# The first B tile moved from the hardware queues to the software queue, and the left half of B loaded by half tiles, in a matmul with RMS norm

## The chip, the cores and the metric

The kernel runs on one core of one Trainium2 chip. The metric is device time in microseconds (us) of one execution. The profile gives a span, from the first to the last instruction of one execution; in all profiled runs the timed value of that execution is 1.8 us above its span, so a change of the span is a change of the time.

Names used below. TensorE is the matrix engine (PE in the profile), DVE the vector engine, ACT the scalar engine, POOL the GpSimd engine, SP the sync engine. A *hardware queue* is a queue of DMA transfers issued by SP or ACT; the *software queue* is issued by POOL, and in this kernel every load that converts float32 to bf16 on its way goes by it. A load has *landed* when the last of the 16 DMA engines has written its share.

## The reference

```python
def reference(a, b, gamma, eps):          # a, b: 2048 x 2048 float32
    x = np.matmul(a, b)
    rms = np.sqrt(np.mean(x ** 2, axis=-1, keepdims=True) + eps)
    return (gamma * x / rms).astype(np.float32)
```

## The kernel before

The output has 16 row blocks of 128 rows. The first four are the *head*: they are multiplied while B is still being loaded, so that TensorE has work from the start. The contraction of 2048 is cut into 8 tiles of 256 rows (kp 0 to 7). In the left half (output columns 0 to 1023), each stage needs 512 KB of A and 1 MB of B, both counted as float32 in memory; in the right half only the 1 MB of B. After the head about 160 us of products follow, which read B from on-chip memory.

How the first tile comes in, before the change. The A tile of kp 0 is one load on the sync queue. The B tile of kp 0 comes as two float32 loads on the scalar queue and is cast to bf16 by DVE and ACT:

```python
    nc.sync.dma_start(out=a0f, in_=a[0:HB * P, 0:W2].rearrange("(r p) k -> p r k", p=P))
    for t in range(2):
        nc.scalar.dma_start(out=b0f[t], in_=b[t * P:(t + 1) * P, 0:HALF])
```

All other tiles come by the software queue, one load of 1 MB for each tile of B (512 KB once written as bf16):

```python
    def load_b(j, kp):
        nc.gpsimd.dma_start(
            out=raw[j][kp],
            in_=b[kp * W2:(kp + 1) * W2, j * HALF:(j + 1) * HALF].rearrange(
                "(t p) n -> p t n", p=P))

    def load_head(kp):
        nc.gpsimd.dma_start(out=ah(kp), in_=a[0:HB * P, kp * W2:(kp + 1) * W2] ...)   # cut
        load_b(0, kp)
```

The loop over the left half issues loads four tiles ahead, then the matmuls:

```python
    for kp in range(KP):
        if kp + 4 < KP:
            load_head(kp + 4)
        else:
            load_later(1)           # a tile of the right half, load_b(1, ...)
        ...                         # transpose the next A tile, then the stage's matmuls
```

The last stage of the right half (kp 7) does the two products of a later pair first (`acc<-b,s` and `acc<-early,s` in the profile), then the eight plain matmuls, then one more `acc<-early,s`. That last one closes the head; I use its start as the end of the head.

```python
        if kp == KP - 1:
            for m in (2, 5):
                pair_matmul(m, kp)          # needs the B tile of kp 7
            pair_matmul(1, kp - 1)
        for g, kt in order:
            head_matmul(banks[g], *g, kt)   # eight, two halves of the tile
        ...
            pair_matmul(1, kp)              # the end of the head
```

Eleven warm-up matmuls on zeros run from 1.46 us, so that the throttle grants TensorE its full clock before real work comes.

## Time and profile before

| | us |
|---|---|
| timed, median of the first 3 runs | 222.82 (222.45 to 223.10) |
| timed, median of all 6 runs of the comparison | 222.53 (222.14 to 223.10) |
| span of the profiled execution (itself timed at 222.97) | 221.2 |
| TensorE busy | 210.0, 95% of the span |

From the page of the kernel before, the busy times and three of the DMA queues (queue, kind: packets, MB written, share of the 16 engines' time):

```profile
PE 210.0 (95%) x1035; PEld 97.7 (44%) x1035; DVE 167.4 (76%) x330; ACT 128.1 (58%) x263; POOL 29.4 (13%) x59
...
q0 software_dynamic: 9936, 23.33, 41.7%
q10 hardware_dynamic: 432, 1.31, 2.0%
q8 instruction: 8, 0.13, 0.2%
```

TensorE is 95% busy, which tempts one to think that loads don't matter. They do in the first 57 us. The timeline of TensorE of the kernel before, at the end of the head (start us, duration us, engine, line, operation, out<-in, shapes, count):

```profile
56.44 0.38 PE L289 MATMUL acc<-early,s 128*128 128x512 bf16 x1
56.69 0.59 PE L289 MATMUL acc<-b,s 128*128 128x512 bf16 x2
...
59.05 0.38 PE L289 MATMUL acc<-early,s 128*128 128x512 bf16 x1
```

The last tile of the right half landed at 56.64 us, and the stage that needs it starts at 56.69. The head ends at 59.05. The chain of waits of the kernel before (start us, length us, what) shows the same from the left half: a load to 25.05, and right after it the matmuls that needed it.

```profile
7.35 17.70 DMA b<-in_b_dram
25.05 0.04 issue
25.10 1.67 PE acc L384 x7
```

In the right half a stage takes TensorE about 2.4 us and a tile about 2.5 us to load.

The start of the kernel before, in the timeline of all engines (the bracket is the idle time before the instruction and what ended it):

```profile
5.16 0.74 DVE L158 CAST b<-early 128x512 bf16<-128x512 f32 x1 [1.28 <-DMA early<-in_b_dram]
6.40 0.63 PE L155 MATMUL tbank<-t_left,early 128*128 128x128 f32 x4 [0.53 <-DMA early<-in_a_dram]
7.54 2.88 PE L384 MATMUL acc<-b,head_at 128*128 128x512 bf16 x12
```

The A tile lands at 6.26, the halves of the B tile at 5.13 and 8.68, and the first real matmul starts at 7.54. The rate of the loads in that time, from the view by stretches of the kernel before (stretch, its length, then busy us and instructions of each engine, granted clock, DMA share, GB/s written). The software queue writes bf16, half of what it reads, so 205 GB/s of a B load are 410 GB/s of source:

```profile
5.00:6.00 1.00, 0.87 (x4) 0.10 (x2) 0.74 (x1) 0.62 (x1) 1.00 (x2) 1.00 1.12 337
6.00:7.00 1.00, 0.60 (x6) 0.63 (x7) 0.00 (x0) 0.00 (x0) 1.00 (x10) 1.00 0.78 196
...
12.00:16.00 4.00, 3.94 (x26) 1.93 (x24) 0.69 (x1) 0.58 (x1) 1.46 (x2) 1.00 1.24 205
```

From 6 to 7 us 196 GB/s were written, mostly float32 by the scalar queue, so the loads ran at half of the 410 GB/s that they reach from 12 us on. The change aims at this first stretch.

### The profile page before, as it was taken

The numbers are of one execution on the slowest core, as the hardware profiler recorded it, in microseconds if no ns is written. First come the engines' busy times: TensorE is split into PE (matmuls) and PEld (weight loads), VectorE is DVE, ScalarE is ACT, GpSimd is POOL, SyncE is SP. The second block draws the span as 40 slices with busy tenths as digits, with TensorE's granted clock in tenths as the row PEclk, the third lists the DMA queues.
The fourth block names the chain that finished last, engine by engine and source line by source line (L and its number), as shares of the span: only waits on it lengthen the run. The fifth ranks groups of instructions, "written<-read, shape, count | busy, mean of one in ns | idle before, by whom it ended". The sixth has DMA issues, their size and how long they took to land.

```text
span 221.2 us, 3022 instructions
## 1 busy us (share of the span) xinstructions
PE 210.0 (95%) x1035; PEld 97.7 (44%) x1035; DVE 167.4 (76%) x330; ACT 128.1 (58%) x263; POOL 29.4 (13%) x59
## 2 busy tenths in 40 slices
PE   7899899999999999999999999999999999999950
PEld 2445454444455444444444444444444444444430
DVE  2428789999988898969696639855794759797691
ACT  3110001830698898678945997389738995334570
POOL 7634323220000001200110002000200000000040
PEclk9999999999999999999999999999999999999996
DMA  6999999999938596956799249955798349044045
GB/s 184 223 202 209 203 208 210 211 211 238 426 114 357 187 291 120 316 230 150 219 308 397 79 88 266 367 221 95 187 302 367 69 90 381 32 190 193 1 190 191
DMA packets 36321, 47.13 MB, mean 213 GB/s; under 512 B 21969, under 2 KB 26065, under 8 KB 34897
## 3 DMA queue, kind: packets, MB, share of 16 engines
q0 software_dynamic: 9936, 23.33, 41.7%
q1 hardware_dynamic: 25936, 22.29, 33.6%
q10 hardware_dynamic: 432, 1.31, 2.0%
q8 instruction: 8, 0.13, 0.2%
q14 instruction: 9, 0.07, 0.1%
HBM read 34.60 MB, written 16.78 MB: 232 GB/s over the span
## 4 chain that ended last, share of the span: by engine, by line
PE 83%; DMA 8%; POOL 3%; DVE 2%; issue 1%; ACT 1%; DVEq 0%; ACTq 0%; POOLq 0%
PE acc L289 69%; PE acc L384 12%; DMA b<-in_b_dram 8%; POOL early L105 1%; POOL b L99 1%; DVE x L709 1%; PE tbank L415 1%; PE tbank L172 1%; DVE x L712 1%; ACT sq L307 0%; PE tbank L189 0%; PE acc L189 0%; DVE a L709 0%; ACT sq L778 0%; DVE x L786 0%
## 5 line engine op out<-in xcount | busy, mean ns | idle before, releaser
L289 PE MATMUL acc<-b,s 128*128 128x512 bf16 x408 | 92.1, 379 | 0.0
L289 PEld LDWEIGHTS <-s 128*128 128x128 f16 (+1 forms) x512 | 49.9, 98 | 59.9 <-DVE s L264 0.4
L384 PE MATMUL acc<-b,head_at 128*128 128x512 bf16 x176 | 41.9, 379 | 1.0 <-DMA b<-in_b_dram 0.9
L307 ACT ACTIVATE sq<-x 128x512 bf16<-128x512 f32 x54 | 34.0, 630 | 6.9 <-DVE x L709 3.0
L366 DVE SCALAR_TENSOR_TENSOR x<-x,r,gamma_sb 128x1024 f32<-128x1024 f32 x28 | 34.8, 1281 | 0.7
L223 ACT ACTIVATE sq<-a 128x1024 bf16<-128x1024 f32 x24 | 25.3, 1054 | 2.4 <-DMA a<-in_a_dram 1.9
L384 PEld LDWEIGHTS <-head_at 128*128 128x128 bf16 x176 | 16.8, 98 | 20.6 <-issue 1.9
L246 ACT ACTIVATE head_at<-a,s 128x2048 f16<-128x2048 f32 x10 | 20.0, 1998 | 3.7 <-DVE s L233 3.7
L426 ACT COPY x<-acc 128x512 f32<-128x512 f32 x6 | 3.4, 586 | 25.7 <-PE acc L384 25.7
L289 PEld LDWEIGHTS <-head_at 128*128 128x128 f16 (+1 forms) x112 | 10.9, 98 | 13.2
L289 PE MATMUL acc<-early,head_at 128*128 128x512 bf16 x64 | 14.5, 379 | 0.0
L289 PEld LDWEIGHTS <-at_even 128*128 128x128 f16 x96 | 9.4, 98 | 11.3
L289 PE MATMUL acc<-early,s 128*128 128x512 bf16 x56 | 14.4, 379 | 0.0
L264 DVE TENSOR_TENSOR s<-head_at 128x1024 f16<-128x1024 f16 (+5 forms) x22 | 13.4, 635 | 0.1
L596 DVE TENSOR_TENSOR x<-x,x 128x512 f32<-128x512 f32 x9 | 6.2, 692 | 8.8 <-ACT x L594 8.3
L99 POOL DMA_DIRECT2D b<-in_b_dram x15 | 10.6, 706 | 16.0 <-DMA b<-in_b_dram 13.4
L578 ACT COPY x<-acc 128x512 f32<-128x512 f32 x9 | 5.2, 574 | 11.6 <-PE acc L289 11.5
L289 PE MATMUL acc<-t_left,s 128*128 128x512 bf16 x48 | 11.3, 379 | 0.0
L280 DVE TENSOR_TENSOR b<-b 128x1024 bf16<-128x1024 bf16 x16 | 10.8, 684 | 0.2
L289 PE MATMUL acc<-t_left,head_at 128*128 128x512 bf16 x48 | 10.9, 379 | 0.0
L289 PE MATMUL acc<-t_left,at_even 128*128 128x512 bf16 x48 | 10.8, 379 | 0.0
L289 PE MATMUL acc<-early,at_even 128*128 128x512 bf16 x48 | 10.8, 379 | 0.0
(111 smaller groups left out, 216.7 us busy)
## 6 DMA issues: line engine op xcount, KB each, us to landing
out_dram<-x SPq DMA_DIRECT2D x30, 512.0 KB, 3.8
a<-in_a_dram POOLq DMA_DIRECT2D x10, 1024.0 KB, 8.7
b<-in_b_dram POOLq DMA_DIRECT2D x15, 512.0 KB, 17.5
a<-in_a_dram POOLq DMA_DIRECT2D x4, 512.0 KB, 16.6
early<-in_a_dram POOLq DMA_DIRECT2D x7, 256.0 KB, 14.8
early<-in_b_dram ACTq DMA_DIRECT2D x2, 512.0 KB, 5.9
gamma_sb<-in_gamma_dram POOLq DMA_DIRECT2D x1, 1024.0 KB, 14.8
early<-in_a_dram SPq DMA_DIRECT2D x1, 512.0 KB, 5.5
```

What stands on the lines that cost most here:

```text
L99: nc.gpsimd.dma_start(out=raw[j][kp], in_=b[kp * W2:(kp + 1) * W2, j * HALF:(j + 1) * HALF].rearrange("(t p) n -> p t n", p=P))
L223: nc.scalar.activation(out=junk, in_=a32[mb][:, h * HALF:(h + 1) * HALF], func=ACTF.Square, scale=2.0 ** -8, accum_out=n2[:, h:h + 1])
L246: nc.scalar.activation(out=a16[mb], in_=a32.pop(mb), func=ACTF.Copy, scale=factor.pop(mb))
L264: nc.vector.tensor_tensor(out=sum_of(g, s)[:, lo:hi, :], in0=x[:, lo:hi, :], in1=y[:, lo:hi, :], op=op)
L280: nc.vector.tensor_tensor(out=flat[:, 1:3, :], in0=flat[:, 1:3, :], in1=flat[:, 0::3, :], op=ALU.add)
L289: nc.tensor.matmul(bank, lhsT[:, kp, :], rhs, start=(start and kp == 0), stop=(kp == KP - 1), skip_group_check=not start)
L307: nc.scalar.activation(out=sq[:, 0:CH], in_=src, func=ACTF.Square, scale=inv_sqrt_n, accum_out=msq[mb][:, c:c + 1])
L366: nc.vector.scalar_tensor_tensor(out=x, in0=x, scalar=inverse_of[mb], in1=gamma_sb[:, h * HALF:(h + 1) * HALF], op0=ALU.mult, op1=ALU.mult)
L384: nc.tensor.matmul(bank, head_at[:, kt, r, :], head_rhs(c, kt), start=(kt == 0), stop=(kt == KT - 1))
L426: copy(out=x_chunk(*g), in_=banks[g])
L578: nc.scalar.copy(out=c, in_=one[1])
L596: nc.vector.tensor_tensor(out=t, in0=t, in1=x12, op=ALU.add)
```

## The change

Its intent: start the loads at full rate sooner. The A tile of kp 0 is split over both hardware queues, so that it lands sooner; the B tile of kp 0 goes first into the software queue, which carries half the written bytes and needs no casts. Every left-half tile of B is loaded as two halves of 128 rows, so that a stage can begin on its first half. The identity needed for the transposes is made right after B0's issue, and there are 8 warm-up matmuls in place of 11.

```diff
-    nc.sync.dma_start(out=a0f, in_=a[0:HB * P, 0:W2].rearrange("(r p) k -> p r k", p=P))
-    for t in range(2):
-        nc.scalar.dma_start(out=b0f[t], in_=b[t * P:(t + 1) * P, 0:HALF])
+    for h, queue in enumerate((nc.sync, nc.scalar)):
+        queue.dma_start(out=a0f[:, 2 * h:2 * h + 2, :],
+                        in_=a[2 * h * P:(2 * h + 2) * P, 0:W2].rearrange("(r p) k -> p r k", p=P))
@@ load_b
+        if j == 0:
+            for t in range(2):
+                lo = kp * W2 + t * P
+                nc.gpsimd.dma_start(out=raw[0][kp][:, t, :], in_=b[lo:lo + P, 0:HALF])
+            return
@@
-    load_head(1)
+    load_b(0, 0)
     identity_f = t_left[:, 2, KP - 1, 0:2 * P].bitcast(FP32)
     make_identity(nc, identity_f)
+    load_head(1)
@@
-    for _ in range(11):
+    for _ in range(8):
         nc.tensor.matmul(warm_bank, warm[:, 0:P], warm[:, 0:CH], start=True, stop=True)
@@ transpose_first: the casts go, the copies are shared by DVE and ACT
-        for t in range(2):
-            cast_first = [...]                                     # cut
-            move = [...]                                           # cut
-            for work in (cast_first + move if t == 0 else move + cast_first):
-                work()
+        for t, copy in enumerate((nc.vector.tensor_copy, nc.scalar.copy)):
+            for h in range(2):
+                copy(out=head_at[:, t, 2 * h:2 * h + 2, :], in_=view[t][:, 2 * h:2 * h + 2, :])
```

More of the change, by code (lines that the diff above doesn't have):

```diff
@@ L67 @@
     a0f = early[:, 0:2048].bitcast(FP32).rearrange("p (r k) -> p r k", r=HB)
-    b0f = [early[:, 2048 + t * 2048:2048 + (t + 1) * 2048].bitcast(FP32) for t in range(2)]
     NAH = 6
@@ L156, in transpose_first @@
                                  is_transpose=True, start=(r == 0), stop=(r == HB - 1))
-        for t in range(2):
-            cast_first = [lambda: nc.vector.tensor_copy(out=raw[0][0][:, t, :CH],
-                                                        in_=b0f[t][:, :CH]),
-                          lambda: nc.scalar.copy(out=raw[0][0][:, t, CH:], in_=b0f[t][:, CH:])]
-            move = [lambda h=h: nc.vector.tensor_copy(
-                out=head_at[:, t, 2 * h:2 * h + 2, :], in_=view[t][:, 2 * h:2 * h + 2, :])
-                for h in range(2)]
-            for work in (cast_first + move if t == 0 else move + cast_first):
-                work()
+        for t, copy in enumerate((nc.vector.tensor_copy, nc.scalar.copy)):
+            for h in range(2):
+                copy(out=head_at[:, t, 2 * h:2 * h + 2, :], in_=view[t][:, 2 * h:2 * h + 2, :])
     def transpose_head(kp):
```

## The prediction

> **What bounds the kernel now.** Span 221.2 us in the profile, 222.8 timed. TensorE is busy 95%, but the first 57 us are bound by loads. The timeline and the landings of the software-queue loads show each stage of the head starting where a tile of B lands: B1 lands at 12.26 us and its matmuls start at 12.30, B2 16.08/16.19, B3 20.14/20.18, B4 25.05/25.10 (the one wait that the waits view lists, 0.9 us). The right half does the same to its end: its last tile lands at 56.64, its first matmul starts at 56.69. The other 164 us are TensorE work. So the change is worth what it moves the last right-half landing, no more. A stage of the left half reads 1.5 MB (float32) in 3.8 us, about 410 GB/s of source bytes; TensorE needs 3.9 us for it. A right stage: 2.5 us of loading, 2.4 of TensorE.
>
> **Where loading time is lost.** First packets: scalar queue at 1.8 us, sync queue at 2.5, software queue only at 6.27, although its first load was issued at 1.25 (later, with nothing else in flight, 1.24 us pass from issue to first packet: 64.33 to 65.57). The software queue starts just as the sync queue's A load has landed (6.26). All queues together move only about 200 GB/s from 2 to 4 and 6 to 8 us. At 410 GB/s throughout, the same 21 MB would need a start at about 3.8 us.
>
> **What the change does.** Source bytes stay equal. 1 MB of B leaves the hardware queues and goes first in the software queue, which carries it as bf16, so four casts go (DVE 0.74 + 0.43, ACT 0.62 twice). The A load is halved over both hardware queues. Nine more POOL issues (estimate 0.55 us each, from the 512 KB A loads) fit: POOL is idle 2 to 3 us of each 3.9. Eight loads in flight are still 4 MB, 10 us of work.
>
> I expect: A landed at 4.2 to 4.8 (now 6.26); the software queue delayed behind it, first packets about 4; first half of B0 near 5.7 to 6.3; first real matmul about 6.2 (now 7.54). Half-tiles let a left stage begin 1.3 us before its second half lands, so TensorE then runs its left stages nearly at its own pace, about 3 us ahead of now at 25 us. Most of that is given back: from the first right-half tile on, loads bind again. Their gain is the equivalent start, 3.8 to about 3.0: **0.8 us**. The Trainium skill ("DMA: Bandwidth & Descriptors", Issuing engines are not separate DMA queues) says all queues share the same 16 engines and only interleave; the trace's constant 410 GB/s agrees.
>
> Warm-ups: the clock is granted fully from 5.26 us, 3.8 us after the first warm-up; eleven end at 5.86, eight end at about 4.9. If the grant comes later, stage 0 runs at half speed (up to 3 us), mostly hidden by the right half's waits.
>
> **Prediction.** 222.0 us, 8 in 10 within 220.9 to 223.5. Faster by over 2%: 0.02; within 2%: 0.96; slower: 0.02.
>
> **What would show it.** Right: software packets before 5 us; last right-half tile landing near 55.8 and its matmul with it; the waits view showing new TensorE waits for B in the right half (2 us or more), none in the left. Wrong: (a) the software queue's first packet still after 6 us, so its start is a fixed latency: then B0 lands after 7.5, all loads slip by 1 us, about 223.9; (b) mixed queues running at 200 GB/s longer; (c) a full clock only after 8 us; (d) the sum of landings moving earlier but TensorE's gain surviving past 57 us.

## More of the kernel before

Where TensorE enters the right half, in the timeline of the kernel before:

```profile
40.25 1.89 PE L384 MATMUL acc<-b,head_at 128*128 128x512 bf16 x8
```

## The result, and the profile after

The changed kernel took 222.79 us, median of 6 runs (222.58 to 223.08), against 222.53 us for 6 runs of the kernel before. The ratio is 1.0009, with a 95% interval of 0.9993 to 1.0025. Ratios here are the mean time of one kernel's fast runs over the mean of the other's of the same rounds, so not quite the ratio of the quoted medians. In a second session (the run named r1_after) it took 222.64 us, ratio 1.0018 [0.9991, 1.0046]. The two are the same within the noise; if there is any difference, the changed kernel is 0.1 to 0.3 us slower, by the medians. The 0.8 us that I had expected it to gain are not there.

From the page of the kernel after:

```profile
PE 209.3 (95%) x1012; PEld 98.2 (44%) x1032; DVE 165.6 (75%) x326; ACT 127.4 (58%) x263; POOL 32.5 (15%) x68
...
q0 software_dynamic: 10336, 23.86, 43.2%
q10 hardware_dynamic: 416, 0.52, 0.7%
```

The work moved as intended: 0.5 MB more through the software queue, 0.8 MB less (written) through the scalar queue q10, 9 more POOL instructions, DVE 1.8 us less busy. Now the start, in the timeline of the kernel after:

```profile
1.24 1.25 POOL L101 DMA_DIRECT2D b<-in_b_dram  x2 [0.79 <-POOLq L811]
4.85 1.06 PE L160 MATMUL tbank<-t_left,early 128*128 128x128 f32 x4
6.55 1.99 PE L383 MATMUL acc<-b,head_at 128*128 128x512 bf16 x7
8.84 1.24 PE L383 MATMUL acc<-b,head_at 128*128 128x512 bf16 x5 [0.30 <-DMA b<-in_b_dram]
```

The A halves land at 4.13 and 4.41, the B halves at 6.35 and 8.80. The transposes start 1.55 us sooner, the first real matmul 0.99 us sooner (6.55 against 7.54). But the second half of B0 lands at 8.80, no sooner than before (8.68). The stretches of the kernel after say why:

```profile
5.00:6.00 1.00, 1.00 (x7) 1.00 (x6) 0.06 (x1) 0.00 (x0) 1.00 (x2) 1.00 0.84 80
6.00:7.00 1.00, 1.00 (x6) 0.63 (x5) 0.70 (x2) 0.20 (x1) 1.00 (x3) 1.00 0.90 110
...
12.00:16.00 4.00, 3.61 (x23) 1.74 (x23) 0.69 (x1) 0.59 (x1) 2.00 (x4) 1.00 1.24 205
```

From 5 to 7 us only the software queue carries data, the engines are counted as 84 to 90% busy, and yet they write 80 and 110 GB/s, that is 160 to 220 GB/s of source, half of what the same queue does from 12 us on. The stretch at half rate that I read in the kernel before, and put down to two kinds of queues mixing, is still there with one queue.

At the other end, the timeline of TensorE of the kernel after (the first line is where it enters the right half), and what its chain of waits shows there:

```profile
39.38 1.67 PE L383 MATMUL acc<-b,head_at 128*128 128x512 bf16 x7
...
55.82 0.38 PE L288 MATMUL acc<-early,s 128*128 128x512 bf16 x1
56.47 0.59 PE L288 MATMUL acc<-b,s 128*128 128x512 bf16 x2 [0.26 <-DMA b<-in_b_dram]
...
58.84 0.38 PE L288 MATMUL acc<-early,s 128*128 128x512 bf16 x1
```

```profile
35.99 20.43 DMA b<-in_b_dram
56.42 0.04 issue
56.47 0.81 PE acc L288 x3
```

The rule of the kernel before holds: the last tile lands at 56.42, its matmuls start at 56.47. TensorE enters the right half 0.87 us ahead of before (39.38 against 40.25), waits for loads there, and closes the head 0.21 us ahead (58.84 against 59.05). The rest of the span is the same work: 162.2 us after the start of that last matmul in both. From the start of the right half to the last stage TensorE took 17.09 us, against 16.44 before, so 0.65 us of its lead of 0.87 us went back into waiting: from the fourth right tile on each stage starts within 0.1 us of its tile's landing (46.29 for 46.19, then 48.70 for 48.65, and so on). The list of waits of TensorE up to 60 us in the kernel after shows only the larger ones (engine, line, waited for: us in total, times, longest):

```profile
PE acc L383 <- DMA b<-in_b_dram: 0.3, 1, 0.3
PE acc L288 <- DMA b<-in_b_dram: 0.3, 1, 0.3
```

A second trace of the same kernel (r1_after) has the last landing at 55.89, the head's end at 58.30 and a span of 220.5 (timed 222.29). A second trace of the kernel before (r2_before) has 56.48, 58.90 and 221.0 (timed 222.81). One kernel's last landing moves by a few tenths of a microsecond from run to run, and the change is of that size. So single traces can't size it; I compare many.

### The profile page after: what moved, and what is told of

It reads as the page before. It is cut to its first block, busy times and chain, and to the rows that moved or that the text cites. A ratio compares the mean times of both kernels' runs of the same rounds, so it can differ in the third digit from the quotient of the medians.

```text
span 221.0 us, 3009 instructions
## 1 busy us (share of the span) xinstructions
PE 209.3 (95%) x1012; PEld 98.2 (44%) x1032; DVE 165.6 (75%) x326; ACT 127.4 (58%) x263; POOL 32.5 (15%) x68
## 4 chain that ended last, share of the span: by engine, by line
PE 68%; DMA 23%; DVE 2%; POOL 2%; issue 2%; ACT 1%; DVEq 0%; ACTq 0%; POOLq 0%
PE acc L288 67%; DMA b<-in_b_dram 18%; DMA early<-in_a_dram 5%; POOL b L101 1%; DVE x L708 1%; PE acc L383 1%; POOL early L109 1%; DVE x L711 1%; ACT sq L306 0%; PE tbank L188 0%; PE acc L188 0%; DVE a L708 0%; ACT sq L777 0%; DVE x L785 0%; DVE x L789 0%
## 5 line engine op out<-in xcount | busy, mean ns | idle before, releaser
L577 ACT COPY x<-acc 128x512 f32<-128x512 f32 x9 | 5.2, 573 | 11.5 <-PE acc L288 7.7
L130 POOL COPY pace<-x 128x1 f32<-128x1 f32 x4 | 1.3, 322 | 66.6 <-DVE x L604 65.1
```

What stands on the lines that cost most here:

```text
L577: nc.scalar.copy(out=c, in_=one[1])
```

## The experiments

Two theories for the first runs: **Theory A**: the time is the landing of the last right-half tile plus a constant; the change starts the loads sooner by less than I thought, and half tiles cost some of it. **Rival B**: TensorE's own chain from a cold start (fewer warm-ups, a later full clock) sets the time, and the loads are bystanders. Each edit below is against the kernel after unless said otherwise. All runs gave the right result. The timed runs were of the fast state, but for one of the kernel before (254.18 us), which is left out; the three kernels that ran once (e4, e7, e8) have an unknown state.

This table collects what the runs gave. "Landing" is when the last right-half tile of B landed, "head end" the start of the last head matmul, both in the profiled execution; the timed median is over the fast runs of the same session, with the ratio to the kernel before.

```
run                landing  head end  span    timed (runs)   ratio [95%]
before             56.64    59.05     221.2   222.53 (6)
r2_before          56.48    58.90     221.0   222.47 (5)     0.9998 [0.9985, 1.0010]
after              56.42    58.84     221.0   222.79 (6)     1.0009 [0.9993, 1.0025]
r1_after           55.89    58.30     220.5   222.64 (6)     1.0018 [0.9991, 1.0046]
e1_warm11          55.80    58.22     220.4   222.46 (6)     0.9998 [0.9984, 1.0013]
e2_whole_tiles     56.14    59.10     221.3   222.28 (4)     0.9993 [0.9974, 1.0012]
e3_extra_load      56.92    59.34     221.6   223.80 (4)     1.0052 [1.0035, 1.0069]
e4_second_first    56.04    58.94     221.1   222.92 (1)
e5_right_halves    56.16    58.35     222.6   224.31 (6)     1.0083 [1.0058, 1.0109]
e7_hold_after_b0   60.32    63.25     225.5   227.24 (1)
e8_b0_after_a0     58.55    60.96     223.2   224.98 (1)
e9_spaced_to_3     56.31    58.72     220.9   223.05 (6)     1.0034 [0.9998, 1.0070]
e10_spaced_to_7    56.21    58.62     220.8   222.64 (4)     1.0021 [0.9985, 1.0057]
e11_before_halves  56.43    58.85     221.0   222.91 (6)     1.0019 [1.0006, 1.0032]
```

And this one is worked out from the trace's DMA records: MB of source that had been read by a given time (a packet of the software queue's B loads counts double, since it writes half of what it reads). From 20 to 50 us the kernel before reads 12.46 MB, 0.415 MB in a microsecond, which turns a lead in MB into one in time.

```
by              5 us   7 us   10 us  12 us  20 us  50 us
before          0.84   1.38   2.47   3.28   6.56   19.02
r2_before       0.82   1.40   2.52   3.33   6.61   19.08
e11_before_halves 0.86 1.40   2.50   3.30   6.53   18.90
after           1.05   1.43   2.62   3.42   6.70   19.12
r1_after        1.05   1.49   2.68   3.48   6.73   19.16
e1_warm11       1.02   1.44   2.57   3.37   6.64   19.07
e2_whole_tiles  1.07   1.52   2.72   3.50   6.78   19.25
```

### Is it the loads, or TensorE's cold start? (e1_warm11, e3_extra_load)

e1 restores the eleven warm-ups:

```diff
-    for _ in range(8):
+    for _ in range(11):
```

> The changed kernel with eleven warm-ups again. Theory A (the last right-half tile of B binds, landed at 56.42 us after the change): the clock is granted sooner than 7.19 us and stage 0 is shorter, but the right half still starts its last stage where that tile lands; time within 0.15 us of the changed kernel (222.8). Rival B (TensorE's own chain, cold in stage 0, sets the time): 0.3 to 0.6 us faster than the changed kernel.

Measured: 222.46 us, ratio 0.9998 [0.9984, 1.0013]; against 222.79 and 222.64 for eight warm-ups. The intervals overlap. By time alone this run doesn't decide between the theories: it is 0.33 us below the first median of the kernel after, which is inside what Rival B expected, and 0.18 us below the second, which is outside both. The traces favour Theory A. The head ended at 58.22, against 58.30 in the closest trace with eight. The spacing of the first matmuls, 0.427 us at half clock and 0.216 at full, shows when the clock was granted: 5.25 us in this run; with eight warm-ups 7.19 in one trace and 4.71 in another. The trace with the late grant spaced its first real matmul by 0.426 us, and ends its head at 58.84, 2.4 us after its last landing like the rest. What follows: in the traces a landing, not the cold start, holds up the last stage with either number of warm-ups. A small effect of the warm-ups on the time, up to about 0.3 us, is not excluded.

e3 adds one load of 512 KB, of no use to anyone, in front of the first right-half tile:

```diff
         else:
+            if kp == KP - 4:
+                nc.gpsimd.dma_start(out=gamma_sb[:, 0:HALF], in_=b[0:P, 0:HALF])
             load_later(1)
```

> The changed kernel plus one load of 512 KB that nobody needs, in the software queue ahead of the right half. At 411 GB/s of source bytes that is 1.28 us. Theory A: 1.1 to 1.3 us slower than the changed kernel, last right-half landing near 57.7 us. Rival B: under 0.6 us slower, TensorE having slack there.

Measured: 223.80 us, 1.0 to 1.2 us above the kernel after; 512 KB at 0.415 MB/us are 1.26 us. In its profiled run, one of its fastest (223.33), the last stage of TensorE begins where the last tile lands, at 56.92 us. The timeline of TensorE of e3:

```profile
56.97 0.59 PE L288 MATMUL acc<-b,s 128*128 128x512 bf16 x2
...
59.34 0.38 PE L288 MATMUL acc<-early,s 128*128 128x512 bf16 x1
```

The landing is sooner than the 57.7 that was expected; it was one trace, and the four times (223.33 to 224.07) agree better with the expectation. What follows: Theory A's rule holds. Bytes added to the loads of the head come back in the time nearly one for one. Over all traces it reads: in ten of the fourteen, the span is 164.5 to 164.6 us above the last landing. The exceptions are e2, e4 and e7, where TensorE's own work came last (0.5 to 0.6 us after the landing; in e7 the clock had also been at half from 18.20 to 21.61 us), and e5, below. Rival B is not needed for the result, but it is not far off either: TensorE is close behind the loads. Its matmuls before the last stage begin 0.22 us apart, so it could have begun that stage at 56.66 in the kernel before (56.44 + 0.22, against 56.69) and at 56.04 in the kernel after (55.82 + 0.22, against 56.47).

### What do the half tiles cost? (e2_whole_tiles, e11_before_halves, r1_after, r2_before)

e2 keeps the new start, but loads tiles 1 to 7 whole again:

```diff
-        if j == 0:
+        if j == 0 and kp == 0:
             for t in range(2):
```

> The changed kernel, but contraction tiles 1 to 7 of the left half of B by one load each again (B0 stays in halves). Theory A: no more than 0.2 us of change in time, since bytes and order are the same and the landing of the last right-half tile stays near 56.4 us; left stages wait for whole tiles. Rival B: left stages start about 1 us later and stay later, 0.5 to 1 us slower than the changed kernel.

e11 does the opposite: the kernel before, with only its left tiles 1 to 7 loaded by halves (the edit is against the kernel before):

```diff
     def load_b(j, kp):
+        if j == 0:
+            for t in range(2):
+                lo = kp * W2 + t * P
+                nc.gpsimd.dma_start(out=raw[0][kp][:, t, :], in_=b[lo:lo + P, 0:HALF])
+            return
```

> The kernel before with only its loads of contraction tiles 1 to 7 of the left half of B made by halves; first pair by hardware queues, eleven warm-ups as before. Theory A (loads bind at the end of the right half, bytes unchanged): the waits of 0.9 us for B in the left half go, and as much is waited in the right half or lost; time within 0.3 us of the kernel before. If splitting has a gain or cost of its own: 0.5 us or more off it.

r1 and r2 repeat the two kernels unchanged, to see the noise:

> The changed kernel unaltered, timed again beside the experiments of this call and with a second trace. Both theories: 222.8 us within 0.4. The span should again be the end of the head (its last matmul on right-half tiles) plus 162.2 us, as in the changed kernel (58.84 and 221.0), the kernel before (59.05 and 221.2) and the run with eleven warm-ups (58.22 and 220.4).

> The kernel before, timed against itself: the noise of the comparison, and a second trace of its head. Its first trace came from a run of 222.97 us, at the upper end of its 17 runs (222.14 to 223.19). If its last right-half landing (56.64 us there) varies from run to run with how far the slowest DMA engine lags, this trace shows it elsewhere, 55.9 to 56.6 us, with the end of the head plus 162.2 us giving the span again; ratio 1.000 within 0.2%.

Measured: these four make a square.

| timed median, us | whole tiles | half tiles |
|---|---|---|
| old start | 222.53 (before; repeat 222.47) | 222.91 (e11) |
| new start | 222.28 (e2) | 222.79 (after; repeat 222.64) |

By these medians half tiles cost 0.3 to 0.5 us on either row, and the new start gains 0.1 to 0.3 us in either column (the ratios, each within its session, give 0 to 0.2). But the cells come from different sessions, and e1 (222.46, new start, half tiles, eleven warm-ups), timed beside e2, is only 0.2 us above it. e11's own cost lies between its two expectations. Of the differences from the kernel before only e11's is outside its noise (1.0019 [1.0006, 1.0032]); e2 by itself is not separated from before, nor from after. The repeat of the kernel before against itself gave 0.9998 with an interval of 0.13% either way. The direction of all four agrees with the table of source bytes, which was not used to make the square: by 50 us e11 is 0.12 to 0.18 MB behind the kernels before (0.3 to 0.4 us), e2 is 0.17 to 0.23 MB ahead (0.4 to 0.6 us), and the three traces with the new start and half tiles are 0.0 to 0.14 MB ahead (0 to 0.3 us). The half tiles lose, in bytes, what the start wins.

The bytes are not the landing, however. A tile has landed only when the last of the 16 DMA engines is done with it, and in each trace one or two engines lag. For the last right-half tile, worked out from its 16 semaphore updates:

```
                  mean engine done   last engine done (the landing)
before, r2        55.05, 54.92       56.64, 56.48
e11               55.33              56.43
e2                54.49              56.14
after, r1, e1     54.84, 54.73, 54.90  56.42, 55.89, 55.80
```

The mean engine tells the same story as the bytes: 0.3 to 0.4 us later in e11, about 0.5 us sooner in e2, 0 to 0.3 us sooner with the new start and half tiles. The last engine, to which the time is tied, is 0.9 to 1.65 us behind the mean and doesn't follow it: in e11 it is no later than in the kernel before. So the cost of half tiles in time rests on e11's one comparison of timed runs, and how the lag of the last engine enters is open.

Part of the cost in bytes can be named. In the trace every load ends, on each of the 16 engines, with one 4-byte packet that takes 22 ns. Seven more loads are 7 x 22 ns = 0.15 us of every engine, an estimate from those numbers. It is less than half of what was measured; the rest is not explained.

e2 also shows why whole tiles don't turn their whole lead in bytes into time. In its profiled run, which was its slowest (223.07, the others 222.11 to 222.30), TensorE waited in the left half for whole tiles, and then it was TensorE that came last, 0.6 us after the landing at 56.14. The list of waits, and the timeline of TensorE, of e2:

```profile
PE acc L383 <- DMA b<-in_b_dram: 1.9, 3, 1.1
```

```profile
56.73 0.59 PE L288 MATMUL acc<-b,s 128*128 128x512 bf16 x2
```

### What makes the slow stretch at 5 to 7 us? (e4, e7, e8, e9, e10)

In the slow stretch, many packets of B, each with 4 KB of source, take 0.2 to 0.4 us, single ones up to 2.5 us, where they take 0.17 us later. These runs each take away one possible reason. They were not meant to be fast.

e4 swaps the two halves of B0, in case the rows of the second half were slow to read:

```diff
-            for t in range(2):
+            for t in ((1, 0) if kp == 0 else (0, 1)):
```

> The changed kernel with the two halves of B0 issued in the other order. In every trace so far B0's packets of 4 KB (source) take 0.17 us each up to about 4.75 us and 0.2 to 0.4 us from there to 7 us, while the second half is read. If the rows of the second half are slow: it is read first, slow from 3.5 to about 5.5 us, and the first half then at 0.17 us a packet. If it is the time or what runs then: no change of the slow stretch, 4.7 to 7 us, now on the first half.

Measured: the slow stretch did not move. One of the stretches of e4:

```profile
6.00:7.00 1.00, 0.76 (x4) 0.46 (x3) 0.70 (x2) 0.20 (x1) 1.00 (x3) 1.00 0.95 92
```

92 GB/s, against 110 in the kernel after. It is not those rows. (Its one timed run, 222.92, has TensorE as the last to come, since the first matmuls had to wait for the later half.)

e8 lets POOL issue B0 only after A0 has landed:

```diff
-    load_b(0, 0)
     identity_f = ...
     make_identity(nc, identity_f)
+    nc.gpsimd.tensor_copy(out=hold, in_=a0f[:, 0, 0:1])
+    load_b(0, 0)
     load_head(1)
```

> The changed kernel, but POOL waits for the A load (landed 4.1 to 4.5 us) before it issues B0, so that B0's packets start near 5.6 us and POOL writes descriptors for the following loads right behind. Bound to the time since the start: slow only up to about 7 us, both halves mixed. Bound to B0's second half: fast first half to about 6.9 us, slow second half from 7 to 9 us. Bound to POOL writing descriptors: slow for both halves, to about 10 us. In all cases the last right-half landing is 1 to 3 us later than 56.4 us and the time later by the same.

Measured: the first software packets came at 5.42 us, and the slow stretch came later with them. The stretches of e8:

```profile
6.00:7.00 1.00, 0.76 (x4) 0.46 (x3) 0.69 (x2) 0.21 (x1) 1.00 (x2) 1.00 1.07 172
7.00:8.00 1.00, 0.00 (x0) 0.00 (x0) 0.00 (x0) 0.44 (x2) 1.00 (x3) 1.00 0.90 127
9.00:10.00 1.00, 1.00 (x5) 0.39 (x4) 0.00 (x0) 0.00 (x0) 0.61 (x1) 1.00 0.77 102
```

So it is not bound to a moment after the program's start, and it doesn't need the hardware queues: those were long done.

e7 lets POOL go silent after B0's issue, until the first half of B0 has landed:

```diff
     make_identity(nc, identity_f)
+    nc.gpsimd.tensor_copy(out=hold, in_=raw[0][0][:, 0, 0:1])
     load_head(1)
```

> The changed kernel, but POOL waits after the identity until the first half of B0 has landed, so it writes no descriptors between about 3 and 6 us. If POOL's descriptor writing (3.0 to 7.4 us) slows the packets: B0 is read at 0.17 us a packet throughout, both halves landed by 6.5 us, and the slow stretch is gone or moves behind 6 us. If it is a matter of time since the start or of B0's rows: still slow from 4.7 us to the end of B0.

Measured: with POOL silent B0 came in at nearly full rate. The stretches of e7:

```profile
5.00:6.00 1.00, 0.74 (x7) 0.59 (x6) 0.66 (x2) 0.23 (x1) 0.00 (x0) 1.00 1.02 164
10.00:12.00 2.00, 0.98 (x11) 0.56 (x10) 0.01 (x1) 0.00 (x0) 2.00 (x4) 1.00 1.30 197
12.00:16.00 4.00, 2.65 (x11) 0.87 (x9) 0.69 (x1) 0.58 (x1) 2.23 (x12) 1.00 1.02 113
```

164 GB/s from 5 to 6 us where the kernel after wrote 80 (after 6 us little of B0 is left). Summed over the packets from 4 to 7 us, the time above 0.17 us each fell from 19.4 to 6.7 us. But B0 did not land sooner: its second half was done on the first engine at 6.40 and on the last at 8.78, since single early packets of 0.9 to 1.3 us had put one engine behind. And a slow stretch then appeared on B1, at 11.5 to 15.3 us, after POOL had issued several loads in a row (the last line, 113 GB/s). This formed a new theory: POOL, while it writes the descriptors of many loads one after another, slows the transfers.

e9 and e10 test it. They put a memset of about 0.4 to 0.6 us on POOL before each issue, up to tile 3 (e9) or 7 (e10), so that the issues come slower:

```diff
+    def pad(kp, n):
+        if 1 <= kp <= 3:                   # e10: 7
+            nc.gpsimd.memset(x_slot[7][:, 0:n], 0.0)
@@ load_b, left half
+                pad(kp, 600)
@@ load_head
+        pad(kp, 400)
```

> The changed kernel, with a memset of a tile that nobody needs yet (estimate 0.4 to 0.6 us of POOL, from its 0.23 us for 128x128) before each of POOL's issues for contraction tiles 1 to 3, so that descriptors are written at about the rate at which they are read and not in one go from 3.0 to 7.4 us. If that burst of descriptor writing slows the packets: B0 read at 0.17 us a packet, its second half landed near 7 us instead of 8.8, last right-half landing 55.3 us or sooner, time 222.1 or less. If the slow stretch comes from something else: still 4.7 to 7 us, same landings within 0.3 us, time 222.5 to 222.9.

> The same spacing for all of the left half, contraction tiles 1 to 7, so that no burst fills the eight places in flight later. If bursts slow the packets: as with spacing to tile 3, or better by up to 0.5 us if a later burst had cost anything. If not: no gain, or a loss where a memset holds an issue back.

Measured: POOL was spread out as meant, one issue in about a microsecond, and the stretch was as slow as before. The timeline of POOL and the stretches of e9:

```profile
4.15 0.62 POOL L99 MEMSET x<- 128x600 f32 x1
4.69 0.54 POOL L106 DMA_DIRECT2D b<-in_b_dram  x1
```

```profile
5.00:6.00 1.00, 1.00 (x7) 1.00 (x6) 0.06 (x1) 0.00 (x0) 1.00 (x3) 1.00 1.01 104
6.00:7.00 1.00, 1.00 (x6) 0.70 (x5) 0.69 (x2) 0.21 (x1) 1.00 (x3) 1.00 1.06 127
```

104 and 127 GB/s against 80 and 110: still about half of 205. The summed time above 0.17 us a packet from 4 to 7 us is 16.3 us; the runs that start just as the kernel after does (after, r1, e2, e3) have 14.7 to 19.5. And from 8 to 10 us, with POOL issuing at the same pace, e9 wrote 207 to 212 GB/s. The theory of the burst falls. The times, 223.05 (with single runs to 225.49) and 222.64, are no better than the kernel after's. Single runs 0.9 to 2.4 us above their median occur in this group, once in e5 and once in r1_after (224.44), and in none of the 50 runs of the kernel before, but for one of 254.18; why is open too.

What stays open: the cause of the slow stretch. What the runs say is only this. With the new start it begins 1 to 2.5 us after the software queue starts from empty with further loads queued behind, lasts 2 to 4 us, moves with that start (e8, e7), and does not depend on which half of B0 comes first (e4) or on the pace of POOL's issues (e9, e10). It does not need the software queue's data either: with the old start (before, r2, e11) the scalar queue's packets of B take 0.2 to 0.4 us on average from 2 to 3.5 us, and again 0.2 to 0.3 us from about 5 to 7 us, while the first software packet comes only at 6.27 to 6.42. Packets of A beside them, from 5 to 6 us, take 0.05 us as elsewhere. Most of the slow packets fall while POOL is issuing its first run of loads. Only e7 silenced POOL for a time; the summed excess there fell to about a third and not to nothing, so that POOL has a part in it is neither shown nor excluded.

### Can the waits of the right half be removed? (e5_right_halves)

If a landing holds the last stage up, halves in the right half too should let TensorE start it sooner. e5 loads all of B by halves and reorders the right stages so that the matmuls of the first half come first:

```diff
     def load_b(j, kp):
-        if j == 0:
-            for t in range(2): ...
-            return
-        nc.gpsimd.dma_start(out=raw[j][kp], ...)
+        for t in range(2):
+            lo = kp * W2 + t * P
+            nc.gpsimd.dma_start(out=raw[j][kp][:, t, :],
+                                in_=b[lo:lo + P, j * HALF:(j + 1) * HALF])
@@ stream_right
+        for n, (g, kt) in enumerate(order):
+            if kp > 0 and n == len(plain):
+                pair_matmul(2, kp)
+                pair_matmul(1, kp - 1)
             ...                                       # cut: the other orders go
```

> The changed kernel with the right half of B by halves too, and the right stages' matmuls ordered so that the second half is needed 1.3 us after the first. Theory A: this takes the wait at the end of the right half away, and what TensorE is ahead at its start (0.87 us: 39.38 against 40.25) stays: 0.5 to 0.8 us faster than the changed kernel, about 222.1. Rival B: no gain, within 0.2 us of it.

Measured: the head ended at 58.35, 0.49 us before the kernel after's, with no wait for loads left in the right half. The time got worse: 224.31 us, ratio 1.0083 [1.0058, 1.0109]. The gain met two new waits. First, TensorE now outran ACT and DVE, which prepare row block 4; it waited 0.39 us for them and was back at the schedule of the kernel after. The timeline of TensorE of e5, then of the kernel after:

```profile
63.65 0.62 PE L183 MATMUL tbank<-identity_h,head_at 128*128 128x128 f16 x8 [0.39 <-DVE head_at L238]
...
77.42 1.90 PE L283 MATMUL acc<-b,s 128*128 128x512 bf16 x8 [0.69 <-DVE s L258]
```

```profile
63.62 0.62 PE L188 MATMUL tbank<-identity_h,head_at 128*128 128x128 f16 x8
...
76.54 2.75 PE L288 MATMUL acc<-b,s 128*128 128x512 bf16 x12
```

That is a matter of e5's order, not a limit for every kernel: e5 computes a pair's product later in its stage, ACT begins to copy it at 57.25 us (56.88 in the kernel after), and so ACT starts on row block 4 at 58.69, no sooner than the kernel after (58.70). The traces of r1 and e1, with the old order and heads that end as early (58.30 and 58.22), kept their lead to the end of the span. Second, POOL's next load of A was late. The timeline of POOL of e5, of POOL of the kernel after, and of ACT of e5:

```profile
64.49 1.56 POOL L119 DMA_DIRECT2D a<-in_a_dram  x1 [11.29 <-DVE s L227]
```

```profile
64.11 0.53 POOL L124 DMA_DIRECT2D a<-in_a_dram  x1 [14.64 <-DVE s L230]
```

```profile
72.09 1.06 ACT L217 ACTIVATE sq<-a 128x1024 bf16<-128x1024 f32 x1 [1.75 <-DMA a<-in_a_dram]
```

The issue took 1.56 us in place of 0.53, the load landed at 72.00 in place of 69.17, ACT waited 1.75 us for it, and TensorE 0.69 us at 77.42; with the work that then slipped behind it, e5 lost 2.0 us against its own head (164.2 us from the head's end to the span's end, in place of 162.2). An instruction fetch of 8 KB began at 64.74, in the middle of the slow issue; that the one caused the other is argued, not shown by a run of its own.

## Why the prediction was right or wrong

The time was inside the range, and nearly all of the weight was on "within 2%", where it fell. That says little for its reasons: the range is 2.6 us wide, and the time of the kernel before lies in it too. The point, 222.0, was 0.8 us too low, and the gain that it stood for did not appear. By the steps of the prediction:

- **"The change is worth what it moves the last right-half landing, no more."** Right. Span minus last landing is 164.5 us before (221.2 - 56.64) and 164.6 after (221.0 - 56.42), and e3's extra bytes came back as time. But "the right half does the same to its end" was misread: before the change only the last right stage starts as its tile lands, and in the profiled run TensorE was there just as late (56.66 against 56.69; 56.22 against 56.53 in r2). Both chains had to move for a gain; TensorE's moved by 0.6 us (56.66 to 56.04), the last landing by 0.2.
- **A landed at 4.2 to 4.8; software packets about 4; first half of B0 5.7 to 6.3; first matmul about 6.2.** Nearly right: 4.41, 3.50, 6.35, 6.55 (6.87 in the second trace).
- **"At 410 GB/s throughout, the same 21 MB would need a start at about 3.8 us ... Their gain is the equivalent start, 3.8 to about 3.0: 0.8 us."** This is the step that failed: a term of the sum that was too large. I read half rate from 6 to 8 us in the kernel before, thought that it came from hardware and software queues mixing, and let it go with the mixing. It stayed, from 5 to 7 us, with one queue alone. Summed over the packets of B up to 12 us, the time above 0.17 us each was 15 to 16 us in the two traces of the kernel before, about 1 us for each of the 16 engines, and 21 us, 1.3 us for each, in the two of the kernel after: the loss that I meant to save was still paid. The lead in source bytes, 0.22 MB (0.5 us) at 5 us, was 0.03 to 0.11 MB (0.1 to 0.3 us) at 7 and about 0.14 MB (0.35 us) at 12.
- **"Nine more POOL issues ... fit" and "Source bytes stay equal."** True of POOL (0.53 us each), but I gave the extra loads no cost on the DMA engines. The source bytes of e2 and e11 and the times put it at 0.2 to 0.5 us, of which 0.15 can be named. That is about the size of the lead that was left, 0.35 us, and fits the nothing that was measured; that it is the reason is argued, since single landings scatter as much.
- **"About 3 us ahead of now at 25 us."** Wrong. Stage 4 of the left half began at 24.23 against 25.10, 0.87 us ahead. Before the change the waits of TensorE for B added to 0.9 us in the view that lists them; half tiles can't give back more than was waited, plus the sooner first matmul. The prediction's own stage lengths said so, 3.8 us of loading against 3.9 of TensorE.
- **Waits of 2 us or more in the right half.** Wrong in size for the same reason: 0.65 us in all, of which the view lists one wait of 0.26.
- **Last landing near 55.8.** 56.42 and 55.89 in two traces, and 55.80 in e1. Before: 56.64 and 56.48.
- **Warm-ups "mostly hidden by the right half's waits".** Right in effect. One trace had its clock at 7.19 us and nothing came of it.
- **Warning (b), "mixed queues running at 200 GB/s longer".** The rate was what happened, the reason was not: they weren't mixed.
- **The base.** The trace that I subtracted from was timed at 222.97, while the kernel's median is 222.5. Subtracting from a slow trace hid part of the error.

On the Trainium skill's part in this: "DMA: Bandwidth & Descriptors", section "Issuing engines are not separate DMA queues", says that DMAs of all issuing engines run on the same 16 engines and interleave. The traces agree as far as they can show it: from 3 to 4 us in the kernel after, packets of the sync, scalar and software queues run side by side. The steady 410 GB/s of source, which the prediction gave for it, is no test, since from 12 us on one queue alone carries the loads. The section doesn't say that one queue alone runs at the full rate from its first packet, and I took it so.

## What to carry to other kernels

When a stretch of a trace runs below its rate, take away the suspected cause in one experiment before you count the stretch as a gain; here the suspected mixing went and the slow stretch stayed. Splitting loads so that compute can begin on a half is worth at most the wait that the profile shows for that load, and it may have a price in loading time (0.2 to 0.5 us for seven more loads here), so split only the tiles that are waited for; e2, with halves for the first tile alone, was not separated from the kernel before, and halves for the one later tile that was waited for, tile 4, were not run. And before working on a chain that comes last, look for the next one: in the kernel before, TensorE's own chain reached the last stage 0.03 us (0.3 us in the second trace) before the load did.

## What the Trainium skill lacked or had wrong

- **No page has the slow first stretch.** For 2 to 4 us early in the loads, many packets with 4 KB of source take 0.2 to 0.4 us in place of 0.17, on the scalar queue (before) and on the software queue (after, where 80 to 110 GB/s were written in place of 205). Its cause is open.
- **"DMA: Bandwidth & Descriptors", Specifications**, gives about 1 us to the first byte of the software path. Alone the queue took 1.24 us from issue to first packet (64.33 to 65.57 in the kernel before). Behind hardware-queue loads issued before it, it took 2.26 us (1.24 to 3.50, after) and 5.0 us (1.25 to 6.27, before, as the sync queue's A landed at 6.26). The page doesn't have that delay.
- **The same page, "Anatomy of one DMA"**, calls the semaphore write of a DMA essentially free, about one cycle. In these traces each load ends with a 4-byte packet of 22 ns on each of the 16 engines, an estimate of 0.15 us for seven more loads. Seven more loads in the stream went with 0.3 to 0.4 us more (e11 over before, 1.0019 [1.0006, 1.0032]); how much of that these packets make is not shown.
- **No page says what instruction fetches do to the loads.** They share the DMA engines: 8 fetches of 16 KB in each run (the q8 line of the page), each 0.9 to 1.4 us on one engine. In the kernel before, the spread between the first and the last engine to land a tile was 0.4 to 0.8 us up to the fetch at 21.5 us, and 1.8 us on the next B tile (23.23 to 25.05) and from there on; in r2, 0.5 to 0.7 and then 1.5 us. A load has landed only when its last engine has, so this fits the one wait of 0.9 us in its left half; no run tested it.
- **"TensorE: Matmul & The Clock Gate", What's actually happening**, speaks of a free-running activity window of about 3.4 us, and has the moment of the full clock vary by 0.5 us either way. The window fits the traces, the small spread does not: with eight warm-ups that begin at 1.46 us, and gaps in TensorE's work after them, the full clock came anywhere from 4.3 to 7.5 us (ten traces, 3.2 us between the first and the last). With eleven it came from 4.8 to 5.3 (four traces).
